# Query loads of the first attention half on ScalarE's queue, and a later planned landing for retention's rows

## The chip, the cores and the metric

The kernel runs on one core of a Trainium2 chip. A core has a matrix engine (TensorE, PE in the profile), a vector engine (VectorE, DVE), a scalar engine (ScalarE, ACT), a general engine (GpSimd, POOL) and an engine for synchronisation and transfers (SyncE, SP). Each engine runs its own list of instructions in order, and engines wait for each other through semaphores. DMA transfers are issued by an engine's queue and then carried by the core's DMA engines. The metric is the device time of one execution in microseconds.

## The reference

One layer of a streaming encoder. A normalised input is projected by one weight matrix into queries, keys, values and gates of two branches. Branch A is a differential attention with 4 heads: two softmaxes over 64-wide halves of each head, of which the second is subtracted, under a mask that is causal by chunks of 64. Branch B is a retention with 4 heads of 128, in chunks with a running state. Both branches are gated, projected, merged and projected again. This is done for a prompt of 2048 positions, and for 64 further positions of a stream with 4096 cached keys (the sample).

```python
h = rmsnorm(x, norm_g) @ w_in                          # layer_inputs
qa, ka, va, za, qb, kb, vb, zb, ga, gb = jnp.split(h, _split_points(), axis=-1)
qa = rmsnorm(qa.reshape(B, T, H_A, 2, DK_A), qn_g)
...
s = jnp.einsum('bqhcd,bkhcd->bhcqk', q, k) * (DK_A ** -0.5)   # diff_attention
s = s - slopes * dist                                  # chunk-causal mask follows
p = jax.nn.softmax(s, axis=-1)
a = p[:, :, 0] - lam * p[:, :, 1]
o = jnp.einsum('bhqk,bkhe->bqhe', a, v)
...
s = jnp.einsum('bnthd,bnshd->bnhts', qc, kc) * d_intra # retention_prompt
intra = jnp.einsum('bnhts,bnshe->bnthe', s, vc)
cross = jnp.einsum('bnthd,nbhde,ht->bnthe', qc, r_before, xi)
o = intra + cross
...
m = ga * (oa @ w_oa) + gb * (ob @ w_ob)                # layer_output
y = x + m @ w_out
```

The float32 products are formed of rounded parts: a weight tile `ws` is split into a high part `wh` and a low part `wl`, an input into `xh` and `xl`, and three matmuls give one product (`wh,xh`, `wl,xh`, `wh,xl`).

## The kernel before

**Stages.** By the trace, the projections of the prompt's first half (its first 1024 positions) and the sample's attention run up to about 586 us. From about 593 us the prompt's attention follows, interleaved with the rest of the projections and with retention: the first half up to about 1040 us, the second half to about 1425 us; a stage of quadrant products (line 1564) up to about 1530 us, and the output side to the end. An attention task takes 256 queries (index p: 0 to 3 in the first half of the prompt, 4 to 7 in the second) of one head h.

**Loads.** All transfers of the kernel before go through SyncE's queue: `ld` (line 279) issues a load and `st` (line 284) a store. One query group (`load_q`, line 1805) is four DMAs of 128 KB, which fill two halves of the 128 partitions twice (`qT_57` and `qT_58` are the two query matrices in device memory, written earlier by the projections). There are two query buffers. `q_loader` calls it for each head and p; for the first head, the groups p = 0 and 1 come from `load_head`. The first half has 16 groups, 64 DMAs, and the second half as many.

**Semaphores of transfers.** The transfers share eight semaphores in the order in which the program issues them, whichever queue issues. In the built program a DMA waits for the landing of the one that used its semaphore before, in most cases eight issues back.

**What sets the order.** The class `Hybrid` writes the program by a planner. Its tasks are generators; `loop` (line 194) always continues the ready task of the lowest priority number. It keeps a planned clock for each engine (`self.pe`, `self.act`, `self.dve`, `self.pool`) and adds to them with `P`, `A`, `V` and `G`. `A(n, ready, extra)` adds 0.84 n + 165 + extra ns to ScalarE's clock. A task yields the planned time at which it may go on, and in `ld` a load is planned to land 2600 ns after its issue plus its size over a rate. The orders of TensorE, ScalarE and VectorE are the order in which the planner wrote the instructions; those of SyncE and GpSimd are set by the layer beneath, which schedules them among the others. `FIRSTQ` adds 4000 ns to the planned landing of the first head's queries of the first half. Buffers (`take`, `give`) and rows of a common arena (`grab`, `drop`) carry planned times too.

**What stands around the change.** At about 593 us the memory of the earlier stage is given over, and the first keys, queries and weight pieces are loaded into it. ScalarE copies results of the running transposed projection (`transposed`, line 1426, copies in `q_copy`, line 1589, profile line 1591; two PSUM buffers `mm`) out of PSUM, makes the exponentials of the softmax (line 1917), the high part of the probabilities (`ath`, line 2003), and casts weight pieces (`wh`, line 727). The low part of a weight piece (`wl`, line 748) is computed by GpSimd. GpSimd also computes `r_y` (line 1745) for the attention's output norm and, for each retention block that isn't the first, the multiply `row<-row` (line 2329) of the loaded queries by a table. A retention block (`ret_block`, line 2310) takes 128 positions: it loads `row<-qbT`, `row<-kbT` and `row<-vbN`, waits for their planned landing, and goes on to the multiply on GpSimd, four matmuls (line 2334), four transposes (line 2339) and more.

Of the kernel before, what the change touches and what calls it, by code (L numbers as in the profile page):

```python
# [8 lines left out]
F32 = mybir.dt.float32  # L9
# [34 lines left out]
LAND = 2000.0  # L44
# [128 lines left out]
class Hybrid:  # L173
# [102 lines left out]
            return self.nc.vector, self.V  # L276
        return self.nc.gpsimd, self.G

    def ld(self, dst, src, nbytes=0):
        self.nc.sync.dma_start(dst, src)  # L280
        self.dma = max(self.dma, self.pe) + nbytes / 300.0
        return self.dma + DMA_LAT

# [1521 lines left out]
    def load_q(self, h, p):  # L1805
        t0 = 256 * p
        yield from self.take("q")
        q = self.sb(self.ap, [128, 4, 256], "q", dt=F32R)
        for j in range(2):
            qj = self.qT[j][h, :, t0:t0 + 256].rearrange("(c d) t -> d c t", c=2)  # L1810
            for o in (0, 64):
                t = self.ld(q[o:o + 64, 2 * j:2 * j + 2].bitcast(F32), qj, 1 << 17)
        self.qs.append((q, t if h or p > 3 else t + FIRSTQ))

    def q_loader(self, half):
# [497 lines left out]
    def ret_block(self, k, t0, r, first):  # L2313
# [9 lines left out]
        self.ld(qt, self.qbT[:, :, t0:t0 + r].rearrange("h p t -> p h t"), 1 << 18)  # L2323
        self.ld(kt, self.kbT[:, :, t0:t0 + r].rearrange("h p t -> p h t"), 1 << 18)
        t = self.ld(vb, self.vbN[t0:t0 + r, :], 1 << 18)
        yield max(t, self.t_rt)
        tx = 0
        if not first:
            nc.gpsimd.tensor_mul(qx, qt, self.rxi[:, :, :r])
# [3 lines left out]
        for h in range(4):  # L2333
            nc.tensor.matmul(s3[:, h, :], kt[:, h, :], qt[:, h, :], start=True, stop=True)
            t = self.P(512)
# [38 lines left out]
        if first:  # L2374
            nc.vector.tensor_copy(state, up)
            t = self.V(512, tu)
        else:
            for h in range(4):
# [3 lines left out]
                t = self.V(128, max(tu, to))  # L2382
# [3 lines left out]
        o, sq = vx[:r, 512:1024], qk[:r, 0:512]  # L2386
# [11 lines left out]
        t = self.V(80)  # L2398
# [3 lines left out]
        t = self.V(632, t2) + SLACK  # L2402
# [3 lines left out]
        for h in range(4):  # L2406
            nc.tensor.transpose(tp[:, r * h:r * h + r], o[:, 128 * h:128 * h + 128], self.ident[:r, :r])
            t = self.P(256)
        res = qk[:, 0:4 * r]
        nc.scalar.copy(res, tp)  # L2410
        t = self.A(4 * r, t)
        self.give(bank, t)
        yield t
        for h in range(4):
            rh = res[:, r * h:r * h + r]
            d3 = self.obT[h].rearrange("p (g c) -> p g c", c=GW)
            if r == 128:
                g0, c0 = t0 // 256, t0 % 256
                t = self.st(d3[:, g0, c0:c0 + 128], rh, 1 << 16)
            else:  # L2420
                t = self.st(d3[:, :, 256:GW], rh.rearrange("p (g c) -> p g c", c=8), 1 << 17)
# [778 lines left out]
```

## Time and profile before

| | |
|---|---|
| median of 3 runs | 1893.64 us (1892.21 to 1895.02) |
| the profiled execution | 1894.89 us |
| its span | 1893.1 us |
| TensorE busy | 1869.9 us, 99% |
| VectorE, ScalarE, GpSimd busy | 1341.6, 973.9, 670.9 us |
| mean granted TensorE clock | 0.999 |

In the profile, a timeline row holds the start, the time from the first to the last of the group, the engine, the line, the operation with its tiles (`out<-in`, buffer numbers left out), the count, and in brackets the idle time ahead of it with what released the engine. SPq is SyncE's queue, whose rows give the time that an issue holds the queue, not the transfer's. A row of waits holds who waited, for whom, the total in us, how many times, and the longest. A row of the chain holds its start, its length and what it was. "To landing" is the time from the issue until the data is there.

### The profile page before, as it was taken

What the parts mean: (1) busy time and instruction counts of PE and PEld (TensorE: products, weight loads), DVE (VectorE), ACT (ScalarE), POOL (GpSimd) and SP (SyncE); (2) the same over time, 40 slices, a digit from 0 to 9 for tenths busy, and PEclk for the clock granted to TensorE, in tenths of its full rate; (3) what the DMA queues carried; (4) which work ended last, traced back from release to release, by engine and by line L of the source; (5) the groups of instructions that cost most, each with busy time, mean ns of one, the idle gap of its engine ahead of it and who ended that gap; (6) DMA issues with size and microseconds to landing.
All of it is one profiled execution on the core that took longest, in us unless ns stands there. A gap on an engine that the chain in (4) does not pass through costs nothing.

```text
span 1893.1 us, 33045 instructions
## 1 busy us (share of the span) xinstructions
PE 1869.9 (99%) x11090; PEld 1647.9 (87%) x11090; DVE 1341.6 (71%) x3111; ACT 973.9 (51%) x2266; POOL 670.9 (35%) x729
## 2 busy tenths in 40 slices
PE   9999999999999899999999999999999999999999
PEld 7788888888888789888888899889999999999887
DVE  6765757657584767886477686578886869977664
ACT  6434544555434566555455565556666536654221
POOL 2420366555552112121311444432122646512442
PEclk9999999999999999999999999999999999999999
DMA  7654555666857867464522854945534998976542
GB/s 254 215 176 123 160 161 180 180 196 195 248 178 200 233 194 213 126 201 123 168 69 83 230 138 133 227 130 139 143 103 138 276 256 280 269 236 206 171 156 78
DMA packets 402556, 340.09 MB, mean 180 GB/s; under 512 B 85329, under 2 KB 348625, under 8 KB 401362
## 3 DMA queue, kind: packets, MB, share of 16 engines
q1 hardware_dynamic: 402386, 337.97, 61.4%
q8 instruction: 88, 1.44, 0.3%
q14 instruction: 82, 0.67, 0.1%
HBM read 218.27 MB, written 118.75 MB: 178 GB/s over the span
## 4 chain that ended last, share of the span: by engine, by line
PE 86%; DMA 6%; DVE 4%; SPq 1%; ACT 1%; issue 1%; POOL 1%; DVEq 0%; ACTq 0%; POOLq 0%
PE mm L1137 27%; PE mm L989 8%; PE tp L989 4%; PE at L1989 3%; PE s L1877 2%; PE s L1878 2%; PE s L989 2%; PE pv L1969 2%; PE pv L1968 2%; PE pv L1967 2%; PE mm L1564 2%; PE s L2793 1%; PE s L2791 1%; PE s L2792 1%; SPq L280 1%
## 5 line engine op out<-in xcount | busy, mean ns | idle before, releaser
L748 POOL TENSOR_TENSOR wl<-ws,wh 128x512 fp32r<-128x512 f32 x108 | 146.4, 1368 | 210.4 <-ACT wh L727 196.7
L1137 PE MATMUL mm<-wh,xh 128*128 128x512 f32 x504 | 204.2, 405 | 3.0 <-ACT wh L727 3.0
L1137 PE MATMUL mm<-wl,xh 128*128 128x512 f32 x504 | 198.5, 394 | 0.8 <-POOL wl L748 0.8
L1137 PE MATMUL mm<-wh,xl 128*128 128x512 f32 x504 | 198.7, 394 | 0.0
L1137 PE MATMUL mm<-xh,wh 128*128 128x288 f32 (+2 forms) x544 | 179.3, 330 | 0.0
L1137 PE MATMUL mm<-xl,wh 128*128 128x288 f32 (+2 forms) x544 | 175.7, 323 | 0.0
L1137 PE MATMUL mm<-xh,wl 128*128 128x288 f32 (+2 forms) x544 | 175.5, 323 | 0.0
L1917 ACT ACTIVATE row<-row,a_mx 128x1024 f32<-128x1024 f32 (+7 forms) x144 | 150.0, 1044 | 11.3 <-DVE a_mx L1896 11.2
L2005 DVE TENSOR_TENSOR atl<-at,ath 128x512 fp32r<-128x512 f32 (+1 forms) x144 | 92.9, 659 | 74.0 <-ACT ath L2003 73.8
L2003 ACT CAST ath<-at 128x512 fp32r<-128x512 f32 (+1 forms) x144 | 79.2, 564 | 110.4 <-PE at L1989 104.0
L1745 POOL TENSOR_TENSOR r_y<-r_y,r_sq 128x256 f32<-128x256 f32 x32 | 29.8, 931 | 286.0 <-DVE r_sq L1742 210.2
L856 POOL TENSOR_TENSOR wl<-ws,wh 128x256 fp32r<-128x256 f32 x64 | 55.2, 862 | 196.2 <-ACT wh L847 196.0
L1886 DVE CUSTOM_DVE_ANT_0 row<-s,dfar 128x512 f32<-128x512 f32 (+2 forms) x148 | 91.5, 632 | 37.5 <-PE s L1878 36.6
L1137 PEld LDWEIGHTS mm<-wh,xl 128*128 128x128 f32 x504 | 95.0, 188 | 21.6
L1137 PEld LDWEIGHTS mm<-wh,xh 128*128 128x128 f32 x504 | 95.1, 189 | 20.7 <-ACT wh L727 3.3
L1137 PEld LDWEIGHTS mm<-wl,xh 128*128 128x128 f32 x504 | 95.4, 189 | 18.4 <-POOL wl L748 1.2
L1137 PEld LDWEIGHTS mm<-xh,wh 128*128 128x128 f32 x544 | 102.5, 188 | 7.4
L1137 PEld LDWEIGHTS mm<-xl,wh 128*128 128x128 f32 x544 | 102.5, 189 | 7.1
L1137 PEld LDWEIGHTS mm<-xh,wl 128*128 128x128 f32 x544 | 102.4, 188 | 6.7
L1939 DVE SCALAR_TENSOR_TENSOR row<-row,a_w 128x1024 f32<-128x1024 f32 (+5 forms) x88 | 98.8, 1128 | 0.0
L1877 PE MATMUL s<-K,q 128*128 128x512 f32 (+3 forms) x241 | 91.7, 381 | 0.2 <-DVE a_acc L1886 0.2
L727 ACT CAST wh<-ws 128x512 fp32r<-128x512 f32 x111 | 66.9, 617 | 41.0 <-DMA ws<-in_w_in_dram 11.2
(543 smaller groups left out, 6077.3 us busy)
## 6 DMA issues: line engine op xcount, KB each, us to landing
ws<-in_w_in_dram SPq DMA_DIRECT2D x155, 256.0 KB, 3.5
q<-qT SPq DMA_DIRECT2D x128, 128.0 KB, 3.1
K<-kT SPq DMA_DIRECT2D x48, 256.0 KB, 4.6
V<-vN SPq DMA_DIRECT2D x24, 512.0 KB, 5.5
row<-in_x_prompt_dram SPq DMA_DIRECT2D x16, 512.0 KB, 4.5
wz<-in_w_in_dram SPq DMA_DIRECT2D x32, 256.0 KB, 4.2
row<-in_cache_k_T_dram SPq DMA_DIRECT2D x32, 256.0 KB, 3.3
row<-in_cache_v_diff_dram SPq DMA_DIRECT2D x32, 256.0 KB, 3.6
```

Of the source, the lines that this page charges most:

```text
L727: self.nc.scalar.copy(h, st)
L748: eng.tensor_sub(l, st, h.bitcast(F32))
L856: nc.gpsimd.tensor_sub(l[:, cs], src, h[:, cs].bitcast(F32))
L989: nc.tensor.matmul(ps, w[:, c], xs[x][c], start=bool(tag) and c == 0 and i == 0, stop=c == 3 and i == 2, skip_group_check=True)
L1137: nc.tensor.matmul(ps, p, q, start=c == 0 and i == 0, stop=c == KC - 1 and i == 2)
L1877: nc.tensor.matmul(ps, q1s, kk, start=True, stop=False)
L1886: nc.vector.tensor_tensor_reduce(out=row[:, k0:k0 + n], in0=ps, in1=tab, scale=-SLOPES[h], scalar=3.0e38, op0=ALU.add, op1=ALU.min, accum_ ...
L1917: nc.scalar.activation(u, u, AF.Exp, bias=mx, scale=-1.0, accum_out=lp[:, k:k + 1])
L1939: nc.vector.scalar_tensor_tensor(out=u0, in0=u1, scalar=w[:, 0:1], in1=u0, op0=ALU.mult, op1=ALU.add)
L1989: nc.tensor.transpose(at[:, w:w + 128], src, self.ident)
L2003: nc.scalar.copy(ah[:, :w], at[:, :w])
L2005: nc.vector.tensor_sub(al[:, :w], at[:, :w], ah[:, :w].bitcast(F32))
```

## The change

`ld` gets an argument for the queue. `load_q` passes ScalarE's queue for p below 4, the first half of the prompt, and SyncE's for the rest; for each of the DMAs on ScalarE's queue the planner adds 0 + 165 + 435 = 600 ns to ScalarE's planned clock. In `ret_block` the planned landing of the rows gets `LAND`, 2000 ns, on top. Lines behind the edit of `load_q` have numbers larger by 3 in the changed kernel.

```diff
-    def ld(self, dst, src, nbytes=0):
-        self.nc.sync.dma_start(dst, src)
+    def ld(self, dst, src, nbytes=0, queue=None):
+        (queue or self.nc.sync).dma_start(dst, src)
         self.dma = max(self.dma, self.pe) + nbytes / 300.0
         return self.dma + DMA_LAT
...
         q = self.sb(self.ap, [128, 4, 256], "q", dt=F32R)
+        queue = self.nc.sync if p > 3 else self.nc.scalar
         for j in range(2):
             qj = self.qT[j][h, :, t0:t0 + 256].rearrange("(c d) t -> d c t", c=2)
             for o in (0, 64):
-                t = self.ld(q[o:o + 64, 2 * j:2 * j + 2].bitcast(F32), qj, 1 << 17)
+                t = self.ld(q[o:o + 64, 2 * j:2 * j + 2].bitcast(F32), qj, 1 << 17, queue)
+                if p < 4:
+                    self.A(0, self.pe, 435)
         self.qs.append((q, t if h or p > 3 else t + FIRSTQ))
...
         t = self.ld(vb, self.vbN[t0:t0 + r, :], 1 << 18)
-        yield max(t, self.t_rt)
+        yield max(t, self.t_rt) + LAND
         tx = 0
         if not first:
             nc.gpsimd.tensor_mul(qx, qt, self.rxi[:, :, :r])
```

The new clocks move the planner's choices: TensorE's 10790 matmuls are the same ones in another order from the first attention on (about 607 us) until 705 instructions before the end.

On ScalarE, where the first attention opens (about 593 us), the order before is this:

```order
L727 CAST wh<-ws 128x512 x2
L1591 COPY ev<-mm 128x256 x3
L1591 COPY ev<-mm 128x288
L1917 ACTIVATE row,a_lp<-row,a_acc 128x128 x2
L1917 ACTIVATE row,a_lp<-row,a_acc 128x256
```

and in the changed kernel this:

```order
L727 CAST wh<-ws 128x512 x2
L280 DMA q<-qT_57 64x2x256 x2
L280 DMA q<-qT_58 64x2x256 x2
L1591 COPY ev<-mm 128x256
L280 DMA q<-qT_57 64x2x256 x2
L280 DMA q<-qT_58 64x2x256 x2
L1591 COPY ev<-mm 128x256 x2
L1591 COPY ev<-mm 128x288
L1920 ACTIVATE row,a_lp<-row,a_acc 128x128 x2
L280 DMA q<-qT_57 64x2x256 x2
L280 DMA q<-qT_58 64x2x256 x2
L1920 ACTIVATE row,a_lp<-row,a_acc 128x256
```

Three query groups now stand between ScalarE's casts, copies and first exponentials.

On SyncE at the same place, the difference reads:

```order
 L280 DMA K<-kT_60 64x1024
-L280 DMA q<-qT_57 64x2x256 x2
-L280 DMA q<-qT_58 64x2x256 x2
-L280 DMA ws<-in_w_in_dram 128x512
-L280 DMA q<-qT_57 64x2x256 x2
-L280 DMA q<-qT_58 64x2x256 x2
+L280 DMA ws<-in_w_in_dram 128x512 x2
 L285 DMA qbT<-ev 128x256
-L280 DMA ws<-in_w_in_dram 128x512
 L280 DMA dfar<-in_c_dfar_dram 128x1920
```

The two weight pieces follow the keys directly, and the query groups are gone from this queue.

On GpSimd, from the weight pieces around 600 us to the first retention blocks (about 650 us), the order before is this:

```order
L748 TENSOR_TENSOR wl<-ws,wh 128x512 x11
L1745 TENSOR_TENSOR r_y<-r_y,r_sq 128x256
L748 TENSOR_TENSOR wl<-ws,wh 128x512
L1745 TENSOR_TENSOR r_y<-r_y,r_sq 128x256
L2329 TENSOR_TENSOR row<-row 128x512
```

and in the changed kernel this:

```order
L748 TENSOR_TENSOR wl<-ws,wh 128x512 x11
L2332 TENSOR_TENSOR row<-row 128x512
L1745 TENSOR_TENSOR r_y<-r_y,r_sq 128x256
L748 TENSOR_TENSOR wl<-ws,wh 128x512
L1745 TENSOR_TENSOR r_y<-r_y,r_sq 128x256 x2
```

The multiply of the second retention block, which was behind the weight piece's low part, now stands ahead of it. Its input `row<-qbT` is the second such load on SyncE; the transfer that used its semaphore before is, in the changed program, the first DMA of the fifth query group on ScalarE.

## The prediction

> **What bounds the kernel now.** I read the head of the page first: which engine fills the span.
>
> ```profile
> span 1893.1 us, 33045 instructions
> PE 1869.9 (99%) x11090; PEld 1647.9 (87%) x11090; DVE 1341.6 (71%) x3111; ACT 973.9 (51%) x2266; POOL 670.9 (35%) x729
> ```
>
> TensorE is busy in all but 23.2 us of 1893.1. The change computes the same, so the matmuls cost the same unless the granted clock moves: it can win only idle time and slow-clock time, and it loses whatever it adds to them. So next the table by stages, then the waits of TensorE.
>
> ```profile
> 586.00:640.00 54.00, 47.88 (x325) 44.31 (x324) 30.62 (x95) 25.25 (x63) 8.86 (x8) 0.97 0.93 240
> 640.00:1040.00 400.00, 399.83 (x2389) 353.74 (x2388) 292.21 (x822) 222.72 (x527) 80.28 (x75) 1.00 0.52 150
> 1040.00:1400.00 360.00, 356.13 (x2416) 328.78 (x2415) 266.60 (x755) 209.65 (x467) 121.71 (x196) 1.00 0.59 156
> 1400.00:1560.00 160.00, 154.97 (x1207) 151.46 (x1206) 120.98 (x216) 88.40 (x177) 72.00 (x53) 1.00 0.74 214
> ...
> 614.00:618.00 4.00, 1.74 (x10) 1.32 (x10) 1.31 (x4) 0.79 (x2) 2.20 (x2) 1.00 0.64 175
> ...
> 627.00:632.00 5.00, 1.32 (x9) 0.71 (x7) 3.64 (x9) 2.22 (x6) 2.40 (x2) 1.00 1.11 295
> 632.00:636.00 4.00, 3.85 (x14) 3.26 (x15) 1.40 (x3) 1.53 (x3) 0.10 (x1) 0.57 1.11 290
> ```
>
> Columns: window, length, busy time of PE, PEld, DVE, ACT, POOL, then granted clock, DMA share, GB/s. The first attention of the first half opens at 586 to 640: 6.1 us idle there, and the clock falls to 0.57 for 4 us behind the longer stop, another (1 - 0.57) x 4 = 1.7 us. In 640 to 1040 TensorE loses 0.17 us in 400, with ScalarE busy in 223 of them. The waits name the stops:
>
> ```profile
> PE mm L1137 <- ACT wh L727: 3.0, 1, 3.0
> ...
> PE s L2334 <- DMA row<-qbT: 1.8, 1, 1.8
> PE s L2334 <- DMA row<-kbT: 1.8, 1, 1.8
> PE tp L1877 <- DMA q<-qT: 1.5, 1, 1.5
> ...
> PE mm L1137 <- POOL wl L748: 0.8, 1, 0.8
> PE tp L1878 <- DMA q<-qT: 0.8, 1, 0.8
> ```
>
> Two belong to the queries (2.3 us), two to one weight piece (3.8), two to retention's rows in the second half (3.6). Last, the queues at the opening: SyncE, then ScalarE, then GpSimd.
>
> ```profile
> 596.14 2.56 SPq L280 DMA_DIRECT2D q<-qT  x4
> 598.79 0.54 SPq L280 DMA_DIRECT2D ws<-in_w_in_dram  x1
> 599.38 2.79 SPq L280 DMA_DIRECT2D q<-qT  x4
> ...
> 610.50 3.85 SPq L280 DMA_DIRECT2D q<-qT  x4
> ...
> 620.23 4.98 SPq L280 DMA_DIRECT2D q<-qT  x4
> 625.31 0.54 SPq L280 DMA_DIRECT2D ws<-in_w_in_dram  x1
> ...
> 633.71 0.43 SPq L280 DMA_DIRECT2D row<-qbT  x1
> ```
>
> ```profile
> 593.33 1.14 ACT L727 CAST wh<-ws 128x512 fp32r<-128x512 f32 x2 [2.36 <-issue]
> 594.37 0.36 ACT L1591 COPY ev<-mm 128x256 f32<-128x256 f32 x1
> 595.32 0.37 ACT L1591 COPY ev<-mm 128x256 f32<-128x256 f32 x1 [0.58 <-PE mm L1137]
> ...
> 630.14 0.62 ACT L727 CAST wh<-ws 128x512 fp32r<-128x512 f32 x1 [2.53 <-DMA ws<-in_w_in_dram]
> ```
>
> ```profile
> 627.62 1.23 POOL L1745 TENSOR_TENSOR r_y<-r_y,r_sq 128x256 f32<-128x256 f32 x1 [11.43 <-ACT row L1917]
> 630.83 1.27 POOL L748 TENSOR_TENSOR wl<-ws,wh 128x512 fp32r<-128x512 f32 x1 [1.98 <-ACT wh L727]
> 640.77 0.73 POOL L1745 TENSOR_TENSOR r_y<-r_y,r_sq 128x256 f32<-128x256 f32 x1 [8.67 <-DVE r_sq L1742]
> 641.47 1.27 POOL L2329 TENSOR_TENSOR row<-row 128x512 f32<-128x512 f32 x1
> ```
>
> One query group is four DMAs, 2.44 to 2.56 us of SyncE where nothing holds them (0.61 each) and 3.85 or 4.98 where one waits. The weight piece of 625.31 is issued behind such a group, and everything after it hangs on its landing: cast 630.14, residual wl 630.83, matmul 632.1.
>
> **The change part by part.** *Sixty-four query DMAs leave SyncE for ScalarE* (half of the 128; 16 groups). On ScalarE I price an issue as on SyncE, 0.61 us: 64 x 0.61 = 39 us more of an engine that is free for 177 of the 400 us from 640 to 1040. No row shows ScalarE issuing. The ends are nothing at all and 4.98 / 4 = 1.25 us (the longest group); I take 0.61, since the transfers are the same ones. A DMA in this program also waits for the DMA that used its semaphore before it, eight issues back, and with two queues that one may stand on the other. On ScalarE such a wait holds casts, copies and exponentials.
>
> The Trainium skill, "DMA: Bandwidth & Descriptors", section "Issuing engines are not separate DMA queues", says that transfers from all engines run on the same 16 DMA engines, and that a second issuer saves only the issue time. The trace agrees as far as it can: share 0.93 at 586 to 640 leaves no room for more transfers at once.
>
> *The stop on the queries at 614 (2.3 us).* The chain of waits shows its cause: the last DMA of the third group waited for the semaphore of a value load that took 8.5 us.
>
> ```profile
> 604.63 8.48 DMA V<-vN
> 613.13 0.57 SPq L280
> 613.75 2.97 DMA q<-qT
> 616.86 0.35 PE tp L1878
> ```
>
> On ScalarE the third group stands behind the first two exponentials (604), its semaphores come from stores instead, and TensorE reaches this place later itself (next paragraph). I count the wait as removed: -2.3, between -2.3 and 0 (if a store's landing holds the group as long).
>
> *The opening copies.* Group one now stands between the two casts and the copy of 594.37, group two between that copy and the one of 595.32. The copies free the two PSUM buffers of TensorE's running projection, whose next chunk, 24 matmuls, began 0.4 us after the first copy's end (594.73):
>
> ```profile
> 595.12 0.28 PE L1137 MATMUL mm<-xh,wh 128*128 128x256 f32 x1
> 595.24 0.28 PE L1137 MATMUL mm<-xl,wh 128*128 128x256 f32 x1
> ```
>
> At 0.12 us from matmul to matmul a chunk lasts 2.9 us. So the next chunk is late by 2.44 - 0.4 = 2.0 us. The second copy has both groups ahead of it and ends at 595.7 + 4.9 = 600.6; its buffer is wanted when the late chunk ends, 597.1 + 2.9 = 600.0: late by 0.6 more, 1 with a wait for a semaphore. That is +3, between 0 (issue nearly free) and +4.5 (1.25 us for each DMA of the first group: 5.0 - 0.4). Three transposes that the new order puts six matmuls ahead of their old place wait for exponentials behind group three: +1, from 0 to 1.7. So TensorE comes to the weight piece of 627.5 about 3 + 1 - 2.3 = 1.7 us later, at 629.
>
> *The weight piece at 632.* SyncE, rid of the 4.98-us group, issues it about 5 us earlier. But its cast stands on ScalarE behind query group five, and, which decides, GpSimd's order changes: before, r_y, wl, r_y, then retention's multiply (640.77 and 641.47 are the last two); after, retention's multiply comes first, then r_y, then wl. That multiply waits for `row<-qbT` of retention's second block. The DMA of it stands on SyncE with its semaphore taken from group five's first DMA, now ScalarE's. The next row gives the landing.
>
> ```profile
> L280 SPq DMA_DIRECT2D row<-qbT x4: 371/428/527, 632.1 to 649.4; - x4
> ...
> DMA to landing us min/median/max: 1.7/4.2/8.2
> ```
>
> Query DMAs take longer to land in this crowded window than the 3.1 us of the whole run:
>
> ```profile
> q<-qT SPq DMA_DIRECT2D x20, 128.0 KB, 4.8
> ```
>
> Group five went out at about 628 before; between exponentials that ran from 624.5 on, I put its first DMA on ScalarE at 626.5. It lands 4.8 us later, 631.3; the row load issued then lands after the median 4.2, 635.5; multiply 1.27, r_y 1.23 and wl 1.27 make 639.3. Against the 632.1 at which wl was ready before that is +7.2. If the semaphore is free early and the row goes out at 624, GpSimd is done at 624 + 4.2 + 3.8 = 632.0, as before, and the cast decides: behind group five, 626.5 + 4.98 + 0.62, then 1.27 of wl, 633.4, or +1.3 (0 with the group at 2.44). With both at their longest, 631.3 + 8.2 + 3.8 = 643.3, +11. I take +5, nearer to +7.2 than to +1.3, since the semaphore order is written in the program and only its time is open. The delays of the two paragraphs before this lie under it: TensorE waits there until wl is ready, whether it comes at 627.5 or 629. They come out only if wl is early.
>
> The Trainium skill, "TensorE: Matmul & The Clock Gate", section "Part 1: The HAM clock gate (the "warmup" mystery)", says that an idle window of about 3.4 us halves the clock until a busy one has passed. The trace agrees: 0.57 behind the stop of 627 to 632, 1.00 through that of 614. By that rule the longer stop pays the same 1.7 us once, so the sum does not change, while a stop cured saves it.
>
> *Steady part, 640 to 1040.* Eleven groups more on ScalarE, 27 us, hidden by its 177 free us and the reserve that TensorE shows (0.17 us lost); waits for semaphores may put a few exponentials late: 0 to +4, I take +1.5.
>
> *Retention's rows 2 us later in the order.* That gives the loads time: -3.6, the two waits of 1.8; what is done in their stead at the same time is other ready matmuls. Against that, a shifted order meets other loads late: 0 to +3, taken +1.5. Net -2.1, from -3.6 to 0.
>
> *The stretch 1400 to 1560* loses 5.0 us, to VectorE; retention's work can fill or miss it: 0, +-2.
>
> Sum: +5 +1.5 -2.1 +0 = +4.4. The profiled execution took 1894.89, 1.25 above the median, so 1899.3 there and 1893.64 + 4.4 = **1898.0** in the median.
>
> **Rivals.** *Faster: SyncE's relief holds.* All removable losses are 2.3 + 3.8 + 1.7 (clock) + 3.6 = 11.4; with ScalarE's issues covered and the row of qbT landed by 628, so that multiply, r_y and wl end before TensorE's 629 + 2, most of it comes: -11.4 to -5, about 1885 (-11.4 + 3 for the opening copies). For it speaks that 0.17 us are lost in 400 where ScalarE is half idle; against it GpSimd's order. The point that decides: `row<-qbT` of block two landing before 628.
>
> *Same: stops only move.* wl at 635 (+3), retention -3, rest 0: about 1894.
>
> *Slower by more: ScalarE's queue holds whenever it waits on a SyncE transfer.* Were each of the 16 groups to cost TensorE 1 us beyond the sum, 1898 + 11 (eleven steady groups) = 1909. The 0.17 us reserve says that one such delay is swallowed; a row of them in 640 to 1040 would show.
>
> The Trainium skill, "Perfetto Trace Analysis", section "DMA Instruction — HWDGE", says that the sequencer takes a lock for the descriptor generator; by that rule two issuers wait for each other while SyncE issues solidly, which points to this rival. No row of before has a second issuer.
>
> **How the numbers follow.** A measurement tells about 0.2% here, 3.8 us: faster is below 1889.9, slower above 1897.4. Chances: slower as summed 0.37, slower by more 0.10, same 0.22, faster 0.31. The sum lies near the bound, so part of the summed case may fall in the same. The summed case's own range is 1894 to 1904. The range 1884 to 1907 takes the relief's 1885 in and most of the dearer case; a tenth is left at either end.
>
> **What would show it.** Right: in 590 to 604 ScalarE's copies 2 to 3 us late; the wait for q at 614 gone; one stop of 6 to 10 us on wl L748 near 630, the POOL's multiply (now L2332) just ahead of it waiting for `row<-qbT`; a clock of about 0.6 behind it; the waits of s L2334 (now L2337) near 1210 and 1246 gone. Wrong: no stop on wl, 586 to 640 with over 49 us of PE; or idle TensorE in 640 to 1040 waiting for ath or exponentials; or ScalarE's issue far from 0.61 us; or new waits in 1040 to 1400 that take back more than 2 us.

## The result and the profile after

The changed kernel is slower: median 1905.62 us (1903.26 to 1909.38, 6 runs) against 1895.88 us (1892.21 to 1898.03, 6 runs) of the kernel before. The ratio is 1.0054, with a 95% interval of 1.0039 to 1.0070, so about 10 us. The profiled execution took 1905.49 us, its span is 1903.7 us, 10.6 longer than the span before. Time, state of the engines and DMA share by stage (columns as before the change: length, busy time of PE, PEld, DVE, ACT, POOL, clock, DMA share, GB/s):

```profile
586.00:640.00 54.00, 42.05 (x288) 38.13 (x286) 27.81 (x86) 20.54 (x53) 7.82 (x7) 0.95 0.95 240
650.00:1040.00 390.00, 388.82 (x2338) 343.76 (x2337) 272.81 (x798) 215.87 (x514) 74.17 (x71) 1.00 0.51 146
1040.00:1400.00 360.00, 359.12 (x2406) 329.74 (x2406) 263.93 (x741) 208.06 (x462) 126.58 (x199) 1.00 0.61 160
...
636.00:642.30 6.30, 0.75 (x2) 0.24 (x2) 2.12 (x6) 0.00 (x0) 3.16 (x3) 0.50 0.62 166
642.30:646.00 3.70, 3.70 (x9) 3.13 (x10) 1.35 (x3) 2.43 (x6) 0.00 (x0) 0.50 0.49 164
646.00:650.00 4.00, 4.00 (x14) 3.16 (x13) 2.00 (x8) 1.79 (x4) 0.00 (x0) 0.69 0.41 148
```

The opening of the first attention loses 12.0 us of TensorE in 586 to 640 where 6.1 were lost, and 2.3 more until 642.3. Behind that stop the clock is 0.50 and then 0.69, which costs 3.7 x 0.50 + 4 x 0.31 = 3.1 us where 1.7 were lost before. From 1040 to 1400 us the loss falls from 3.9 to 0.9, and from 1400 to 1560 it is 5.3 instead of 5.0. The waits of TensorE in the changed kernel:

```profile
PE mm L1137 <- POOL wl L748: 5.5, 1, 5.5
PE mm L1137 <- ACT ev L1591: 4.9, 3, 2.5
PE mm L1137 <- ACT wh L727: 3.8, 1, 3.8
PE s L2670 <- DVE ga L2683: 1.9, 1, 1.9
```

The stop on q near 614 and both stops on retention's rows near 1210 and 1246 are gone. New are the copies (4.9 us) and one wait on VectorE near 1557 (1.9), and the stop on the weight piece has grown from 3.0 + 0.8 to 3.8 + 5.5 us. The wait near 1557 also costs slow clock:

```profile
1545.00:1570.00 25.00, 23.12 (x177) 22.91 (x176) 13.42 (x26) 10.47 (x26) 8.57 (x8) 0.93 0.86 239
...
1561.00:1563.00 2.00, 2.00 (x11) 2.00 (x10) 1.71 (x5) 2.00 (x7) 0.00 (x0) 0.50 0.73 256
```

A mean clock of 0.93 over 25 us is about 1.7 us lost; before, it was 1.00 there. The chain of waits at the opening shows what made it, from the value loads to wl:

```profile
620.98 7.15 DMA V<-vN
628.13 0.78 issue
628.91 4.73 DMA q<-qT
633.66 5.28 DMA row<-qbT
639.07 0.12 POOL row L2332
...
640.29 0.72 POOL r_y L1745
641.01 1.23 POOL wl L748
642.28 1.22 PE mm L1137 x2
```

A value load that lands at 628.1 frees the semaphore of the fifth query group's first DMA on ScalarE; that DMA's landing frees the semaphore of retention's row load on SyncE; its landing starts GpSimd's multiply; r_y and wl stand behind. But the row itself isn't later than it was. In the kernel before, the same load goes out at 633.71, in its turn behind the other issues on SyncE, and takes this long to land:

```profile
row<-qbT SPq DMA_DIRECT2D x1, 256.0 KB, 6.8
```

So it lands at 640.5 there and at 638.9 here. What is new is that wl stands behind the multiply that waits for it. ScalarE's own rows at the opening:

```profile
594.26 1.93 ACTq L280 DMA_DIRECT2D q<-qT  x3
596.23 0.37 ACT L1591 COPY ev<-mm 128x256 f32<-128x256 f32 x1 [1.56 <-PE mm L1137]
596.51 5.30 ACTq L280 DMA_DIRECT2D q<-qT  x4
601.85 0.65 ACT L1591 COPY ev<-mm 128x256 f32<-128x256 f32 x2 [5.26 <-issue]
...
609.09 5.79 ACTq L280 DMA_DIRECT2D q<-qT  x4
614.93 0.51 ACT L1920 ACTIVATE row<-row,a_acc 128x256 f32<-128x256 f32 x1 [5.67 <-DMA q<-qT]
...
628.91 3.31 ACTq L280 DMA_DIRECT2D q<-qT  x4
...
635.28 0.60 ACT L727 CAST wh<-ws 128x512 fp32r<-128x512 f32 x1
```

Where nothing holds it, an issue takes 1.93 / 3 = 0.64 us of ScalarE. Groups two and three hold ScalarE 5.3 and 5.8 us, more than twice that, waiting for landings of earlier transfers. The cast of the weight piece comes at 635.28; it was at 630.14, although the piece itself now lands a little earlier: it is issued at 621.9 instead of 625.3 and lands at 629.5 instead of 630.1.

### The profile page after: what moved, and what is told of

Read it like the earlier page. It is cut to its first block, busy times and chain, and to the rows that moved or that the text cites. A ratio compares the mean times of both kernels' runs of the same rounds, so it can differ in the third digit from the quotient of the medians.

```text
span 1903.7 us, 32991 instructions
## 1 busy us (share of the span) xinstructions
PE 1873.8 (98%) x11090; PEld 1649.2 (87%) x11090; DVE 1323.7 (70%) x3110; ACT 975.1 (51%) x2266; POOL 674.7 (35%) x730
## 4 chain that ended last, share of the span: by engine, by line
PE 85%; DMA 6%; DVE 5%; issue 1%; ACT 1%; POOL 1%; SPq 1%; ACTq 0%; DVEq 0%; POOLq 0%
PE mm L1137 27%; PE mm L989 8%; PE tp L989 4%; PE at L1992 3%; PE s L1880 2%; PE s L1881 2%; PE s L989 2%; PE mm L1564 2%; PE pv L1972 2%; PE pv L1971 2%; PE pv L1970 2%; PE s L2794 1%; PE s L2796 1%; PE s L2795 1%; DMA q<-qT 1%
## 5 line engine op out<-in xcount | busy, mean ns | idle before, releaser
L748 POOL TENSOR_TENSOR wl<-ws,wh 128x512 fp32r<-128x512 f32 x109 | 151.8, 1405 | 236.8 <-ACT wh L727 202.9
L1137 PEld LDWEIGHTS mm<-wl,xh 128*128 128x128 f32 x504 | 95.6, 190 | 23.2 <-POOL wl L748 6.1
```

Source lines behind the costliest of these rows:

```text
L748: eng.tensor_sub(l, st, h.bitcast(F32))
L1137: nc.tensor.matmul(ps, p, q, start=c == 0 and i == 0, stop=c == KC - 1 and i == 2)
```

## The experiments

Below, "against before" is the ratio to the kernel before on the same chip, turned into us by 1896 us.

**The plan without the queue.** The changed order on TensorE, ScalarE and VectorE, all queries on SyncE:

```diff
-        queue = self.nc.sync if p > 3 else self.nc.scalar
+        queue = self.nc.sync
```

> The changed kernel's plan (charge of 600 ns and later landing kept, so TensorE, ScalarE and VectorE run the changed order), but all query groups stay on SyncE's queue. Theory A (the queue: query groups on ScalarE hold copies and exponentials, and their landing holds the row load that GpSimd waits for): most of the +9.7 us goes, -3 to +2 us against the kernel before, and the stop before wl near 640 is at most as long as before, 4 us. Rival B (the new order of TensorE's work is what costs): +7 us or more stay.

Median 1895.41 us, ratio 0.9996 (0.9986 to 1.0006). In the new order, then, nothing is lost that can be measured: the whole 10 us come with the queue. In this run the layer beneath put GpSimd's multiply back behind wl, so it alone doesn't tell the issues on ScalarE from GpSimd's order.

**The queue without the plan.** The order of before, the queries on ScalarE, neither charge nor later landing:

```diff
-                if p < 4:
-                    self.A(0, self.pe, 435)
...
-        yield max(t, self.t_rt) + LAND
+        yield max(t, self.t_rt)
```

> The order of the kernel before (no charge, no later landing), but the first half's query groups issue on ScalarE's queue. Theory A: slower, +6 to +14 us, with the copies of 594 to 602 late by 2 to 5 us and the stop before the weight piece near 630 longer than 5 us. Rival B (order): within 2 us of the kernel before.

Median 1912.14 us, ratio 1.0093 (1.0079 to 1.0107): +18 us, beyond theory A's range. The stop before wl is there with the same cause, GpSimd's multiply ahead of it:

```profile
639.55 1.26 POOL L2330 TENSOR_TENSOR row<-row 128x512 f32<-128x512 f32 x1 [3.07 <-DMA row<-qbT]
640.77 1.26 POOL L748 TENSOR_TENSOR wl<-ws,wh 128x512 fp32r<-128x512 f32 x1
```

The rest are waits on ScalarE's and VectorE's results that came late: 2.7 us on `ath`, and 3.6 us on VectorE's `row` near 680. The changed kernel doesn't have these two; whether the charge for the issues or the later landing spares them, this run, which leaves out both, doesn't tell.

**The two parts alone.** The later landing without queue and charge:

```diff
-        queue = self.nc.sync if p > 3 else self.nc.scalar
+        queue = self.nc.sync
...
-                if p < 4:
-                    self.A(0, self.pe, 435)
```

> Only the later planned landing of retention's rows (2000 ns), all queries on SyncE, no charge. Theory A: the two waits on row<-qbT and row<-kbT near 1210 and 1246 go, -2 to -4 us against before. Rival: other loads come late in their stead, 0 +-1.5 us.

Median 1900.73 us, ratio 1.0025 (1.0013 to 1.0037): slower by 5 us, a miss for both expectations. The two waits on retention's rows are gone as expected, but the stretch from 1400 to 1560 us, which waits for VectorE, loses 8.8 us of TensorE where it lost 5.0:

```profile
PE s L2668 <- DVE ev L1584: 3.8, 1, 3.8
PE mm L1564 <- DVE ev L1584: 3.5, 2, 2.7
```

```profile
1400.00:1560.00 160.00, 151.20 (x1174) 148.03 (x1173) 119.18 (x242) 87.53 (x175) 64.51 (x49) 0.99 0.65 191
```

From 650 to 1040 it loses 1.8 us where it lost 0.2. So the later landing wins its 3.6 us and the new order gives it back, and more, in stages that the edit does not touch. And the queue with its charge, without the later landing:

```diff
-        yield max(t, self.t_rt) + LAND
+        yield max(t, self.t_rt)
```

> Only the first half's queries on ScalarE's queue with the charge of 600 ns per DMA, no later landing. Theory A: as slow as the changed kernel or slower by what the later landing wins, +8 to +14 us against before, waits on retention's rows near 1210 to 1250 present. Rival (the two parts need each other to do harm: the later landing is what puts GpSimd's multiply ahead of wl): +1 to +5 us.

Median 1921.80 us, ratio 1.0142 (1.0127 to 1.0158): +27 us, worse than both expectations. The opening loses 14.0 us in 586 to 650, as in the changed kernel (14.2), but 650 to 1040 loses 10.2. Waits on retention's rows near 1210 to 1250 did not come back, against what I expected: this plan is a third one. In this plan the later landing is worth 17 us, with the queue on SyncE it costs 5. Its sign belongs to the plan, not to the loads.

**The weight piece's low part on VectorE.** In the changed kernel, one of its wl operations moves, so that GpSimd's wait for the row can't hold it; the counter `nnext` numbers the calls of `next_piece`:

```diff
-            self.next_sub(self.nc.gpsimd, self.G, st, h, l, t, new)
+            self.next_sub(self.nc.vector if self.nnext == 12 else self.nc.gpsimd, self.G, st, h, l, t, new)
```

> The changed kernel; only the low part wl of the one weight piece for which TensorE waits at 636 to 642 is computed by VectorE instead of GpSimd. If GpSimd's wait for retention's row is what holds wl (theory A1), wl is ready about 0.7 us behind its cast, 636.6 instead of 642.2: 5 to 7 us faster than the changed kernel, +3 to +5 us against before. If only the cast on ScalarE counts, or the stop goes on to the next thing that is late (rival), under 2 us are won.

Median 1901.43 us, ratio 1.0025 (1.0014 to 1.0036) against 1.0054: about 5.5 us won of the 10. GpSimd's multiply still waits, until 641.57, but nothing stands behind it that TensorE needs at once:

```profile
629.58 3.97 ACTq L280 DMA_DIRECT2D q<-qT  x4
...
636.61 0.60 ACT L727 CAST wh<-ws 128x512 fp32r<-128x512 f32 x1
```

```profile
641.57 1.28 POOL L2332 TENSOR_TENSOR row<-row 128x512 f32<-128x512 f32 x1 [16.83 <-DMA row<-kbT]
```

The wait on the cast stays, 4.3 us; the cast stands behind the fifth query group and the exponentials that the group held. So wl's place behind the multiply on GpSimd is about one half of the loss, as theory A1 expected.

**The first head on SyncE.** The changed plan, with four groups back on SyncE, twelve on ScalarE:

```diff
-        queue = self.nc.sync if p > 3 else self.nc.scalar
+        queue = self.nc.scalar if p < 4 and h else self.nc.sync
```

> The changed kernel's plan; the first head's four query groups are issued by SyncE, the other twelve by ScalarE. Theory A (all of it happens at the opening): -3 to +2 us against before, and 640 to 1040 us loses under 1.5 us. Rival C (ScalarE held throughout the first half): +4 us or more, lost between 650 and 1040.

Median 1896.64 us, ratio 1.0004 (0.9995 to 1.0013); 650 to 1040 loses 1.2 us, as in the changed kernel. Twelve groups on ScalarE cost nothing that can be measured in this plan. So all of the loss needs some of the first head's groups on ScalarE, and rival C falls here.

**The same, but also in the plan.** Here the first head isn't charged either, so that the order is planned anew (later landing kept):

```diff
-        queue = self.nc.sync if p > 3 else self.nc.scalar
+        queue = self.nc.scalar if p < 4 and h else self.nc.sync
...
-                if p < 4:
+                if p < 4 and h:
                     self.A(0, self.pe, 435)
```

> The later landing, and ScalarE's queue with its charge for the heads 1 to 3 of the first half only; the first head stays on SyncE in plan and queue. Theory A: as e3, -4 to 0 us against before. Rival C (ScalarE's queue costs wherever it is used): slower than the later landing alone by 3 us or more.

Median 1904.43 us, ratio 1.0048 (1.0035 to 1.0060): +9, and about 4 above the later landing alone, which is what rival C's expectation said; theory A's is missed. The order is a new one too, so the 4 us aren't shown to be the queue's alone. In this order the harm of a held ScalarE does show in the steady part:

```profile
761.24 2.93 ACTq L280 DMA_DIRECT2D q<-qT  x2
...
767.18 2.56 ACTq L280 DMA_DIRECT2D q<-qT  x4
769.78 0.60 ACT L1302 ACTIVATE sq<-mm 128x512 f32<-128x512 f32 x1 [3.81 <-PE mm L1137]
```

```profile
770.41 0.69 DVE L1308 TENSOR_TENSOR raw<-mm,gk 128x512 f32<-128x512 f32 x1 [7.61 <-ACT sq L1302]
```

VectorE waits 7.6 us behind two query groups, and TensorE 3.6 us for `row` (line 1942), which VectorE makes right behind it. So rival C's mechanism exists. That it bites only where the order has something urgent behind the group is argued from these two plans, not tested.

**The first two groups on SyncE.** The groups that stood ahead of the copies:

```diff
-        queue = self.nc.sync if p > 3 else self.nc.scalar
+        queue = self.nc.scalar if p < 4 and (h or p > 1) else self.nc.sync
```

> The changed kernel's plan; only the first two query groups (those ahead of the copies of 594 and 595) go back to SyncE. GpSimd's multiply falls back behind wl with it. If the opening copies and GpSimd's order are the loss: no stop on copies at 595 to 602, wl ready near 633, 0 to +3 us against before. If groups three to five on ScalarE do harm by themselves: +6 us or more.

Median 1898.91 us, ratio 1.0015 (1.0006 to 1.0024), +3, within the first expectation. The copies come in time and GpSimd's multiply is behind wl, yet TensorE waits 5.5 us for the cast: here the weight piece itself lands late, and the cast ran as soon as it was there.

```profile
634.09 0.62 ACT L727 CAST wh<-ws 128x512 fp32r<-128x512 f32 x1 [3.58 <-DMA ws<-in_w_in_dram]
```

The opening copies' loss was no loss of its own: without it TensorE reaches the weight piece earlier and waits there. The fifth group is still on ScalarE in this run, and about 7 of the 10 us are gone without moving it: GpSimd's multiply is behind wl, and wl alone now holds TensorE 0.5 us.

**The fifth group on SyncE.** Of the changed kernel only the group whose landing held the row:

```diff
-        queue = self.nc.sync if p > 3 else self.nc.scalar
+        queue = self.nc.scalar if p < 4 and (h, p) != (1, 0) else self.nc.sync
```

> The changed kernel's plan; only the fifth group (second head, first queries), whose landing held the row load, goes back to SyncE. GpSimd's multiply falls back behind wl with it. The opening stops stay (4 us), wl ends as soon behind its cast as GpSimd can, 635 to 638: +3 to +5 us against before, as with wl on VectorE. If the stop before wl stays longer than 7 us in all: +8 us.

Median 1893.28 us, ratio 0.9983 (0.9974 to 0.9992). One group out of 16 moved back takes about 13 us off and makes the kernel a little faster than before: more than expected. The cast comes at 631.06, and wl starts about 1 us behind its end:

```profile
631.94 0.73 POOL L1745 TENSOR_TENSOR r_y<-r_y,r_sq 128x256 f32<-128x256 f32 x1 [8.18 <-DVE a_w L1931]
632.63 1.26 POOL L748 TENSOR_TENSOR wl<-ws,wh 128x512 fp32r<-128x512 f32 x1
641.10 1.28 POOL L2332 TENSOR_TENSOR row<-row 128x512 f32<-128x512 f32 x1 [7.21 <-DMA row<-qbT]
```

```profile
PE mm L1137 <- ACT ev L1591: 4.0, 2, 2.8
PE mm L1137 <- POOL wl L748: 1.7, 1, 1.7
```

The multiply starts as late as ever, 641, and harms nothing where it now stands. Its row load went out at 634.11, with the fifth group on SyncE, and in every run of this document the load leaves SyncE between 633.4 and 637.0. So the group's landing on ScalarE didn't make the row later than it is anyway; the order on GpSimd made the row matter. The opening stops on the copies (4.0 us) are still there, and the kernel isn't slower for them, as the run before this one says from the other side. Two runs that move only some groups back cured the whole loss, with the first head's four groups or with this one: in both, GpSimd's multiply falls behind wl again and the cast comes at 631 to 632.

**One or two groups on ScalarE in the order of before.** Can the queue be had for the stop at 627 to 632 alone?

```diff
+        queue = self.nc.scalar if (h, p) == (0, 3) else self.nc.sync
```

> The kernel before with one query group alone (first head, last queries; 620.23 on SyncE, 4.98 us there) on ScalarE, in the same order. The weight piece behind it on SyncE is issued about 5 us earlier, its cast and wl come in time: the stop of 3.8 us and the slow clock behind it go, -3 to -6 us. If ScalarE is held by the group's semaphores at 620 instead, so that exponentials come late: -1 to +3 us.

Median 1895.78 us, ratio 0.9994 (0.9985 to 1.0003), no gain that can be measured; the first expectation is missed. And with two groups:

```diff
+        queue = self.nc.scalar if h == 0 and 1 < p < 4 else self.nc.sync
```

> The kernel before with the first head's third and fourth query groups on ScalarE, in the same order. If ScalarE's issue is harmless there: the stops on q (2.3 us) and on the weight piece (3.8 us and clock) both go, -5 to -8 us. If the third group holds the first exponentials on ScalarE as it does in the changed kernel (5.8 us at 609): worse than with the fourth group alone by 2 us or more.

Median 1897.32 us, ratio 1.0011 (1.0003 to 1.0020), 3 us worse than with one group. That is the size of the second expectation, but not its cause: TensorE's longest wait is 5.7 us for the cast of the weight piece. The piece was to go out about 5 us earlier, at 620. On SyncE, the run with one group and then the run with two show:

```profile
624.21 2.98 SPq L280 DMA_DIRECT2D ws<-in_w_in_dram  x1
```

```profile
624.65 4.61 SPq L280 DMA_DIRECT2D ws<-in_w_in_dram  x1
```

SyncE is held in the piece's issue until 627 and 629. This is not the wait for the piece's semaphore, which is over when the row starts. In the run with two groups a key load had the semaphore before, and the chain of waits shows its landing, at 624.59, ahead of the piece:

```profile
620.48 4.12 DMA K<-kT
624.65 8.94 DMA ws<-in_w_in_dram
```

What holds the issue itself for 3.0 and 4.6 us stays open. The query groups no longer stand in the way, and yet the piece lands at 631.7 and 633.6, no earlier than in the kernel before (630.1); the casts run at 631.74 and 633.68. The DMA share from 600 to 632 is about the same with and without the groups on SyncE; the lines are those of the kernel before and of the run with two groups:

```profile
600.00:632.00 32.00, 26.03 (x171) 23.38 (x169) 18.23 (x70) 16.37 (x44) 6.14 (x5) 1.00 1.04 265
```

```profile
600.00:632.00 32.00, 26.53 (x175) 23.83 (x174) 18.03 (x69) 14.43 (x40) 5.00 (x4) 1.00 1.02 233
```

The DMA engines are taken throughout in both (and carry less, 233 GB/s, in the second). That they, and not the issue, set when the piece lands is argued from this, not shown: another queue here only moved which transfer was late.

**Both cures in one.** The fifth group on SyncE and wl of that piece on VectorE (the edits of the two runs together):

```diff
+        queue = self.nc.scalar if p < 4 and (h, p) != (1, 0) else self.nc.sync
...
+            self.next_sub(self.nc.vector if self.nnext == 12 else self.nc.gpsimd, self.G, st, h, l, t, new)
```

> Both cures in one: the changed kernel's plan, the fifth query group on SyncE, and wl of the one weight piece on VectorE. If the stop before wl that is left with the fifth group on SyncE (1.9 us) is only GpSimd's time: 1 to 2 us faster than that kernel, -4 to -6 us against before. If the weight piece's landing or its cast is what really comes last there, under 0.7 us are won.

Median 1895.14 us, ratio 1.0001 (0.9992 to 1.0010): no gain over the fifth group alone (0.9983), rather a loss of about 3 us. The 1.7 us on wl became 0.2, and TensorE waits for VectorE a few matmuls later:

```profile
PE s L1880 <- DVE a_acc L1889: 2.5, 3, 2.0
...
PE mm L1137 <- DVE wl L748: 0.2, 1, 0.2
```

In VectorE's order wl stands ahead of the score operations that TensorE's buffers wait for.

## Why the prediction was right, point by point

The direction and the place were right: slower, by one stop on wl near 640 behind GpSimd's multiply, held by a row load that waited for a query DMA on ScalarE. The forecast was +4.4 us, measured were about +10. The median of 1905.6 lies inside the stated 1884 to 1907, but above the 1894 to 1904 of the summed case; the wide range, which took in a dearer rival that wasn't the cause, held it by luck.

One link was read too strongly. The query DMA's landing does release the row load, but the load went out at 633.66, as before (633.71). The prediction let it go out at 624 if its semaphore were free early; no run shows it before 633.4. What turned an old landing into a stop is GpSimd's order, which the prediction also named as what decides.

- *The issue price.* 0.61 us taken, 0.64 measured. What was missed is the holding: groups of 5.3 and 5.8 us, over the 4.98 us that I had as the longest.
- *The opening copies, +3.* Measured 4.9 us of waits, more than the 4.5 given as the most. That these lie under the later stop was right: with the copies in time but the weight piece late (first two groups on SyncE) the stop took their place, and with the copies late (fifth group on SyncE) the kernel wasn't slower.
- *The stop on q, -2.3.* Gone, as counted.
- *The weight piece, +5 between 0 and +11.* This is the term that was mis-sized. The chain came out link by link, but later at each: the fifth group's first DMA at 628.91 instead of 626.5, landed after 4.73 us (4.8 taken), the row after 5.28 (4.2), wl's matmul at 642.28 against 632.15, +10.1. The worked-out value was +7.2; I then went down to +5, because the cast alone gave +1.3. But the two are not alternatives to average: wl waits for the later one, and GpSimd's was the later. The cast, too, was later than taken: it ends at 635.9, and at 637.2 in the run with wl on VectorE, where the prediction's other case has it end at 632.1. In all, 586 to 650 loses 14.2 us of TensorE instead of 6.1; with the slow clock that is 9.5 us more, against the +5.
- *The clock.* I let the longer stop pay the same 1.7 us. It paid 3.1, since the clock was 0.50 for 3.7 us after work resumed and 0.69 for 4 more. The wait near 1557 paid another 1.7, which I had not in view.
- *The steady part, +1.5.* 650 to 1040 loses 1.2 us where it lost 0.2. The size is right, the reason isn't shown: the waits left there are on VectorE's `a_acc`, and the same plan with all queries on SyncE loses 2.8. The dearer rival, ScalarE held throughout, doesn't show here, but it does in another order (the heads 1 to 3 planned anew), where it stopped TensorE for 3.6 us.
- *Retention's rows, -2.1.* The waits went, and 1040 to 1400 wins 3.0 us; a new wait of 1.9 us on VectorE at 1557 takes part of it, and its slow clock more. Net -1 by the stages (-3.0, +0.3, +1.7), inside the range, and by luck: alone, the later landing is slower by 5 us, and on top of the queue and its charge it is worth 17. I had neither in view: an order that differs early differs everywhere.
- *The stretch 1400 to 1560, 0.* 5.3 us lost against 5.0, the wait at 1557 among them.

The sum by the two profiles starts from TensorE's busy time in the changed kernel:

```profile
PE 1873.8 (98%) x11090; PEld 1649.2 (87%) x11090; DVE 1323.7 (70%) x3110; ACT 975.1 (51%) x2266; POOL 674.7 (35%) x730
```

Its idle time went from 23.2 to 29.9 us, by +8.1 in 586 to 650, +1.0 in 650 to 1040, -3.0 in 1040 to 1400, +0.3 in 1400 to 1560, and the rest elsewhere. Its busy time went up by 3.9, of which the slow clock at the opening is 1.4 and that behind 1557 is 1.7. Together this is 6.7 + 3.9 = 10.6, the difference of the spans. The faster rival named its point of decision, the row landing before 628: it landed at 638.9. The weighed page rules stand so.

The Trainium skill, "DMA: Bandwidth & Descriptors", section "Issuing engines are not separate DMA queues", agrees with the two runs in the order of before: with the query groups off SyncE, the weight piece landed no sooner. The Trainium skill, "TensorE: Matmul & The Clock Gate", section "Part 1: The HAM clock gate (the "warmup" mystery)", gives one busy window of about 3.4 us until the clock is back; here it took more: the clock is 0.50 to 648, 0.77 to 649 and 1.00 behind that, so about 6 us after work resumed at 642.3. Nor is the idle window of about 3.4 us, which the prediction cites for the halved clock, needed here: a stop of 1.9 us was enough at 1557, with the clock at 0.50 from 1560 to 1563. There the measurement decides.

The lock of the Trainium skill, "Perfetto Trace Analysis", section "DMA Instruction — HWDGE", isn't seen as a price: ScalarE's three issues from 594.26 on took 0.64 us each while SyncE was issuing keys.

```profile
593.89 3.75 SPq L280 DMA_DIRECT2D K<-kT  x4
```

SyncE's four took 2.40 us before. The fourth now starts only at 597.20, when ScalarE's first query DMA, issued at 593.56, lands after 3.6 us; it takes over that one's semaphore in the built program, which accounts for the longer row without a lock.

What stays open: why the later landing costs 5 us without the queue and is worth 17 us with it was only followed to the stages where the time is lost, not to the choice of the planner that makes it. And the queue with GpSimd's order held as it was before was not tried: each cure by moving groups changed GpSimd's order too. Nearest to it are the run with wl on VectorE, which leaves both the queue and the multiply in place and wins half, and the run with the first two groups on SyncE, which keeps the fifth on ScalarE and wins 7 of the 10 us. Why the layer beneath puts the multiply ahead of wl in some programs wasn't followed.

## What to carry to other kernels

In this kernel a transfer issued by ScalarE cost it the issue time and also the wait for the landing that its semaphore needed: a group of four, 2.6 us at 0.64 each, took up to 5.8, and the work behind it on ScalarE was late. About half of the loss came through an engine that the edit doesn't touch, by a changed order on GpSimd. Before moving loads to another queue, look whether the transfers or the issue are the limit (here the share was 1.0), and follow, in the new order, what each engine has directly behind the moved issue and what has fallen in front of it on the others. Undoing the change for four, two and one of its sixteen groups, under the same plan, found that one group, moved back, undid the whole loss.

## What had not been expected

One query group decided 13 us: on ScalarE 1.0054, on SyncE 0.9983, the queues of the other 15 unchanged; it took GpSimd's order with it. And the retention landing's effect had either sign by plan: +5 us alone, -17 us on top of the queue and its charge, where the two waits that it was made for didn't appear without it either.
